# A batched matrix-vector product: longer pieces per load, y loaded once, one reduce in four moved to GpSimd and ScalarE

One core of a Trainium2 chip (trn2) is used. The metric is the device time of one execution in microseconds, lower is better.

## The reference

```python
def setup_inputs():
    batch, dim_i, dim_j = 32, 512, 1024
    return {"x": randn(batch, dim_i, dim_j) as float32, "y": randn(batch, dim_j) as float32}

def reference(x, y):
    return np.einsum('bij,bj->bi', x, y)          # float32
```

Each of the 32 x 512 results is a dot product of 1,024 elements. The input x has 67.1 MB and each of its elements is used once, so the time cannot be shorter than reading x takes.

## The kernel before

```python
    xp = ctx.enter_context(tc.tile_pool(name="xp", bufs=12))
    yrowp = ctx.enter_context(tc.tile_pool(name="yrowp", bufs=4))
    ybcp = ctx.enter_context(tc.tile_pool(name="ybcp", bufs=3, space=PSUM))
    # ... (cut)
    for b in range(B):
        yrow = yrowp.tile([1, J], fp32)
        nc.sync.dma_start(out=yrow, in_=y[b : b + 1, :])
        ybc = ybcp.tile([P, J], fp32)                 # y[b] on all 128 partitions
        for h in range(J // MM_FREE):
            nc.tensor.matmul(ybc[:, sl], lhsT=ones, rhs=yrow[:, sl], start=True, stop=True)
        for t in range(IT):                           # 4 tiles of 128 rows
            xt = xp.tile([P, J], fp32)
            eng = x_dma_engines[(b * IT + t) % 2]     # SyncE and ScalarE in turn
            eng.dma_start(out=xt, in_=x[b, t * P : (t + 1) * P, :])
            nc.vector.tensor_tensor_reduce(out=scratch, in0=xt, in1=ybc, op0=mult, op1=add,
                                           accum_out=res_sb[:, col : col + 1])   # ... (cut)
    nc.tensor.transpose(res_T_psum, res_sb, identity)  # then one copy and one store
```

A load has 512 KB, one row (4 KB) per partition. A reduce multiplies a tile by the broadcast y and sums along the row, on VectorE.

## Time and profile before

| | before |
|---|---|
| time, median of 15 runs | 180.3 us (179.97 to 181.2) |
| span in the profile | 178.7 us |
| VectorE busy | 157.4 us in 257 instructions |
| rate of the stream in most slices | 408 to 411 GB/s |

The lines are shown and read in the prediction below. In the page of a profile, the first part gives the busy time of each engine (DVE is VectorE, ACT ScalarE, POOL GpSimd, PE TensorE, PEld its weight loads). The second gives each in 40 equal slices of the span, and the bytes per second in the row GB/s. A line of part 5 is a group of equal instructions: line of code, engine, operation, output <- inputs, shapes, count | busy us, mean ns of one | idle us before them and what ended most of it.

### The profile page before, as it was taken

The page shows a single profiled execution, that of the slowest core. Times are in us where ns is not written, and L with a number is a line of the kernel's source. Part 1 is how long each engine was busy: PE and PEld are TensorE (multiplying, and loading weights), DVE is VectorE, ACT ScalarE, POOL GpSimd, SP SyncE. Part 2 cuts the span into 40 slices and gives each one's busy share as a digit, 9 for nine tenths or more (in the row PEclk, how much of TensorE's full clock was granted, in tenths as well). Part 3 has the DMA queues.
Part 4 walks back from the last instruction along what each step waited for, and adds up shares of the span by engine and source line. Part 5 has one row for each costly group of instructions (what it writes and reads, how often), then busy time and mean ns, then how long its engine had stood idle before and what let it go on. Part 6 is the DMA issues. An engine that isn't in the chain of part 4 may idle for free. (4 is left out here: it accounts for less than half of the span.)

```text
span 178.7 us, 1032 instructions
## 1 busy us (share of the span) xinstructions
PE 119.6 (67%) x129; PEld 37.5 (21%) x129; DVE 157.4 (88%) x257; ACT 1.5 (1%) x2; POOL 0.7 (0%) x6
## 2 busy tenths in 40 slices
PE   2586666787666688666678766667969898666001
PEld 1122211122211122221112222221314232111000
DVE  0379899999999999999999999999999999999992
ACT  0000000000000000000000000000000000002000
POOL 1000000000000000000000000000000000000000
DMA  5999999999999999999999999999999999999800
GB/s 182 423 412 409 408 409 409 411 409 408 411 408 410 409 411 411 409 410 410 408 407 402 388 413 401 370 393 415 408 405 364 391 372 409 406 414 409 319 6 15
DMA packets 18646, 67.37 MB, mean 377 GB/s; under 512 B 2096, under 2 KB 2224, under 8 KB 18640
## 3 DMA queue, kind: packets, MB, share of 16 engines
q1 hardware_dynamic: 9424, 33.76, 47.9%
q10 hardware_dynamic: 9216, 33.56, 47.5%
q14 instruction: 5, 0.04, 0.1%
q8 instruction: 1, 0.02, 0.0%
HBM read 67.24 MB, written 0.07 MB: 377 GB/s over the span
## 5 line engine op out<-in xcount | busy, mean ns | idle before, releaser
L68 DVE CUSTOM_DVE_ANT_0 scratch<-xt,ybc 128x1024 f32<-128x1024 f32 x128 | 156.2, 1221 | 17.2 <-PE ybc L55 12.7
L55 PE MATMUL ybc<-yrow,ones 1*128 1x512 f32 x128 | 119.1, 1087 | 44.7 <-DMA yrow<-in_y_dram 41.1
L55 PEld LDWEIGHTS ybc<-yrow,ones 1*128 1x128 f32 x128 | 37.3, 319 | 124.9 <-issue 113.4
L68 DVE DVE_READ_ACCUMULATOR2_ANT res_sb<- 128x1 f32 x128 | 10.5, 82 | 0.0
L80 PE MATMUL res_T_psum<-identity,res_sb 128*128 128x128 f32 x1 | 0.4, 447 | 11.7 <-DVE res_sb L68 11.7
L80 PEld LDWEIGHTS res_T_psum<-identity,res_sb 128*128 128x128 f32 x1 | 0.2, 183 | 13.3 <-issue 13.3
L82 ACT ACT_TABLE_LOAD x1 | 1.3, 1283 | 160.9 <-DMA xt<-in_x_dram 160.9
L40 DVE MEMSET ones<- 1x128 f32 x1 | 0.2, 165 | 0.8 <-PEq L99 0.8
L82 ACT COPY res_T_sb<-res_T_psum 128x128 f32<-128x128 f32 x1 | 0.3, 266 | 13.8 <-PE res_T_psum L80 13.8
masks.py:199 POOL TENSOR_SCALAR_AFFINE_SELECT identity<-identity 128x128 f32<-128x128 f32 x1 | 0.3, 294 | 0.1
masks.py:197 POOL MEMSET identity<- 128x128 f32 x1 | 0.2, 206 | 0.3 <-POOLq L99 0.3
L99 POOL MEMSET const-bfloat16-1.0<- 128x1 bf16 x1 | 0.1, 102 | 0.0
L99 POOL MEMSET const-uint8-127<- 128x1 uint8 x1 | 0.1, 102 | 0.0
L99 POOL MEMSET const-float32-0.0<- 128x1 f32 x1 | 0.1, 99 | 0.2 <-issue 0.2
L99 POOL MEMSET const-float32-1.0<- 128x1 f32 x1 | 0.1, 99 | 0.0
## 6 DMA issues: line engine op xcount, KB each, us to landing
xt<-in_x_dram ACTq DMA_DIRECT2D x64, 512.0 KB
xt<-in_x_dram SPq DMA_DIRECT2D x64, 512.0 KB
yrow<-in_y_dram SPq DMA_DIRECT2D x32, 4.0 KB
out_dram<-res_T_sb SPq DMA_DIRECT2D x1, 64.0 KB
```

The lines of the kernel that those rows point to most:

```text
L40: nc.vector.memset(ones, 1.0)
L55: nc.tensor.matmul(ybc[:, sl], lhsT=ones, rhs=yrow[:, sl], start=True, stop=True,)
L68: nc.vector.tensor_tensor_reduce(out=scratch, in0=xt, in1=ybc, scale=1.0, scalar=0.0, op0=mybir.AluOpType.mult, op1=mybir.AluOpType.add, a ...
L80: nc.tensor.transpose(res_T_psum, res_sb, identity)
L82: nc.scalar.copy(res_T_sb, res_T_psum)
L99: nc = _bacc.Bacc("TRN2", target_bir_lowering=False, num_devices=1)
```

## The change

The intent is to take time from all three things that the loop is made of. Loads become 2 MB, with four consecutive rows (16 KB) per partition. The whole of y is loaded once, and a column of the identity picks the row to broadcast. One of the four reduces of a batch is done as a product on GpSimd and a sum on ScalarE. The last batch keeps 512 KB loads.

```diff
-    xp = ctx.enter_context(tc.tile_pool(name="xp", bufs=12))
+    PACK = 4;  TAIL = 1;  OFFLOAD = 1
+    packs = [PACK] * (B - TAIL) + [1] * TAIL
+    xp = ctx.enter_context(tc.tile_pool(name="xp", bufs=7))
+    yall = consts.tile([B, J], fp32)
+    nc.sync.dma_start(out=yall, in_=y)
...
-                lhsT=ones,
-                rhs=yrow[:, sl],
+                lhsT=identity[0:B, b : b + 1].broadcast_to([B, P]),
+                rhs=yall[:, sl],
+        off = OFFLOAD if b < B - 1 else 0
+        if off:
+            nc.scalar.copy(ysb, ybc)                  # a copy of y in SBUF for GpSimd
...
-            eng.dma_start(out=xt, in_=x[b, t * P : (t + 1) * P, :])
+            src = x[b, t * P * pack : (t + 1) * P * pack, :].rearrange("(p r) j -> p r j", r=pack)
+            nc.sync.dma_start(out=xt, in_=src)
+                if u < off:
+                    nc.gpsimd.tensor_tensor(prod, xt[:, k, :], ysb, mult)
+                    nc.scalar.activation(junk, prod, Copy, accum_out=res_sb[:, col : col + 1])
+                else:
+                    nc.vector.tensor_tensor_reduce(...)   # as before
...
+        if b == g1 - 1:        # groups of up to 8 batches: 4 transposes, 4 strided copies, one store
```

More of the change, by code (lines that the diff above doesn't have):

```diff
@@ L23 @@
     P = 128
-    IT = I // P
-    assert I % P == 0
-    NCOL = B * IT
+    UNITS = I // P
     MM_FREE = 512
+    PACK = 4
+    TAIL = 1
+    OFFLOAD = 1
+    packs = [PACK] * (B - TAIL) + [1] * TAIL
+    groups, start = [], 0
+    for b in range(1, B + 1):
+        if b == B or packs[b] != packs[start] or (b - start) == 8:
+            groups.append((start, b))
+            start = b
     consts = ctx.enter_context(tc.tile_pool(name="consts", bufs=1))
-    xp = ctx.enter_context(tc.tile_pool(name="xp", bufs=12))
-    yrowp = ctx.enter_context(tc.tile_pool(name="yrowp", bufs=4))
+    xp = ctx.enter_context(tc.tile_pool(name="xp", bufs=7))
     ybcp = ctx.enter_context(tc.tile_pool(name="ybcp", bufs=3, space=bass.MemoryType.PSUM))
+    ysbp = ctx.enter_context(tc.tile_pool(name="ysbp", bufs=3))
+    prodp = ctx.enter_context(tc.tile_pool(name="prodp", bufs=3))
     scratchp = ctx.enter_context(tc.tile_pool(name="scratchp", bufs=1))
-    resp = ctx.enter_context(tc.tile_pool(name="resp", bufs=1))
-    outp = ctx.enter_context(tc.tile_pool(name="outp", bufs=1))
-    outpsum = ctx.enter_context(tc.tile_pool(name="outpsum", bufs=1, space=bass.MemoryType.PSUM))
-    ones = consts.tile([1, P], fp32)
-    nc.vector.memset(ones, 1.0)
+    outsbp = ctx.enter_context(tc.tile_pool(name="outsbp", bufs=2))
+    outpsum = ctx.enter_context(tc.tile_pool(name="outpsum", bufs=2, space=bass.MemoryType.PSUM))
+    yall = consts.tile([B, J], fp32)
+    nc.sync.dma_start(out=yall, in_=y)
     identity = consts.tile([P, P], fp32)
@@ L44 @@
     scratch = scratchp.tile([P, J], fp32)
-    res_sb = resp.tile([P, NCOL], fp32)
-    x_dma_engines = [nc.sync, nc.scalar]
+    junk = scratchp.tile([P, J], fp32)
+    res_sb = consts.tile([P, B * UNITS], fp32)
+    gi = 0
+    out_sb = None
     for b in range(B):
-        yrow = yrowp.tile([1, J], fp32)
-        nc.sync.dma_start(out=yrow, in_=y[b : b + 1, :])
-        ybc = ybcp.tile([P, J], fp32)
+        pack = packs[b]
+        ybc = ybcp.tile([P, J], fp32, name=f"ybc{b}", tag="ybc")
         for h in range(J // MM_FREE):
@@ L61 @@
             )
-        for t in range(IT):
-            xt = xp.tile([P, J], fp32)
-            eng = x_dma_engines[(b * IT + t) % len(x_dma_engines)]
-            eng.dma_start(out=xt, in_=x[b, t * P : (t + 1) * P, :])
-            col = b * IT + t
-            nc.vector.tensor_tensor_reduce(
-                out=scratch,
-                in0=xt,
-                in1=ybc,
-                scale=1.0,
-                scalar=0.0,
-                op0=mybir.AluOpType.mult,
-                op1=mybir.AluOpType.add,
-                accum_out=res_sb[:, col : col + 1],
-            )
@@ L79 @@
-    res_T_psum = outpsum.tile([P, NCOL], fp32)
-    nc.tensor.transpose(res_T_psum, res_sb, identity)
-    res_T_sb = outp.tile([P, NCOL], fp32)
-    nc.scalar.copy(res_T_sb, res_T_psum)
-    out_view = out.rearrange("b (t p) -> (b t) p", p=P)
-    nc.sync.dma_start(out=out_view, in_=res_T_sb)
+        off = OFFLOAD if b < B - 1 else 0
+        if off:
+            ysb = ysbp.tile([P, J], fp32, name=f"ysb{b}", tag="ysb")
+            nc.scalar.copy(ysb, ybc)
+        g0, g1 = groups[gi]
+        if b == g0:
+            out_sb = outsbp.tile([8, I], fp32, name=f"outsb{gi}", tag="outsb")
@@ new lines @@
+        for t in range(UNITS // pack):
+            xfull = xp.tile([P, PACK, J], fp32, name=f"x{b}_{t}", tag="x")
+            xt = xfull[:, 0:pack, :]
+            src = x[b, t * P * pack : (t + 1) * P * pack, :].rearrange("(p r) j -> p r j", r=pack)
+            nc.sync.dma_start(out=xt, in_=src)
+            for k in range(pack):
+                u = t * pack + k
+                col = b * UNITS + u
+                if u < off:
+                    prod = prodp.tile([P, J], fp32, name=f"prod{b}_{u}", tag="prod")
+                    nc.gpsimd.tensor_tensor(prod, xt[:, k, :], ysb, mybir.AluOpType.mult)
+                    nc.scalar.activation(
+                        junk, prod, mybir.ActivationFunctionType.Copy,
+                        accum_out=res_sb[:, col : col + 1],
+                    )
+                else:
+                    nc.vector.tensor_tensor_reduce(
+                        out=scratch,
+                        in0=xt[:, k, :],
+                        in1=ybc,
+                        scale=1.0,
+                        scalar=0.0,
+                        op0=mybir.AluOpType.mult,
+                        op1=mybir.AluOpType.add,
+                        accum_out=res_sb[:, col : col + 1],
+                    )
@@ new lines @@
+        if b == g1 - 1:
+            G = g1 - g0
+            tr_ps = outpsum.tile([8, UNITS, P], fp32, name=f"trps{gi}", tag="trps")
+            for u in range(UNITS):
+                nc.tensor.transpose(
+                    tr_ps[:G, u, :], res_sb[:, g0 * UNITS + u : g1 * UNITS : UNITS], identity
+                )
+                t_, k_ = divmod(u, pack)
+                c0 = P * pack * t_ + k_
+                nc.scalar.copy(
+                    out_sb[0:G, c0 : c0 + pack * (P - 1) + 1 : pack], tr_ps[:G, u, :]
+                )
+            nc.scalar.dma_start(out=out[g0:g1, :], in_=out_sb[:G, :])
+            gi += 1
```

## The prediction

> **What bounds the kernel now.** I read the page first (busy shares, the row of slices, the groups), then the table of windows, then the waits of the engines, then the timeline of the last 20 us.
>
> ```profile
> PE 119.6 (67%) x129; PEld 37.5 (21%) x129; DVE 157.4 (88%) x257; ACT 1.5 (1%) x2; POOL 0.7 (0%) x6
> DMA  5999999999999999999999999999999999999800
> GB/s 182 423 412 409 408 409 409 411 409 408 411 408 410 409 411 411 409 410 410 408 407 402 388 413 401 370 393 415 408 405 364 391 372 409 406 414 409 319 6 15
> DMA packets 18646, 67.37 MB, mean 377 GB/s; under 512 B 2096, under 2 KB 2224, under 8 KB 18640
> ...
> L68 DVE CUSTOM_DVE_ANT_0 scratch<-xt,ybc 128x1024 f32<-128x1024 f32 x128 | 156.2, 1221 | 17.2 <-PE ybc L55 12.7
> L55 PE MATMUL ybc<-yrow,ones 1*128 1x512 f32 x128 | 119.1, 1087 | 44.7 <-DMA yrow<-in_y_dram 41.1
> L55 PEld LDWEIGHTS ybc<-yrow,ones 1*128 1x128 f32 x128 | 37.3, 319 | 124.9 <-issue 113.4
> L68 DVE DVE_READ_ACCUMULATOR2_ANT res_sb<- 128x1 f32 x128 | 10.5, 82 | 0.0
> ```
>
> The DMA row is full from slice 1 to slice 36, at 408 to 411 GB/s in most slices. In the later half some fall to 364 to 402. VectorE is nearly as full. Two resources of almost the same length therefore run side by side. The input alone is 32 x 512 x 1024 x 4 B = 67.1 MB, and 67.1 MB at 410 GB/s is 163.7 us. VectorE has 128 reduces, and the timeline shows what each really occupies:
>
> ```profile
> 171.65 1.22 DVE L68 CUSTOM_DVE_ANT_0 scratch<-xt,ybc 128x1024 f32<-128x1024 f32 x1
> 172.79 0.08 DVE L68 DVE_READ_ACCUMULATOR2_ANT res_sb<- 128x1 f32 x1
> 172.91 1.22 DVE L68 CUSTOM_DVE_ANT_0 scratch<-xt,ybc 128x1024 f32<-128x1024 f32 x1
> ...
> 174.17 1.22 DVE L68 CUSTOM_DVE_ANT_0 scratch<-xt,ybc 128x1024 f32<-128x1024 f32 x1
> 175.32 0.08 DVE L68 DVE_READ_ACCUMULATOR2_ANT res_sb<- 128x1 f32 x1
> 175.54 0.45 PE L80 MATMUL res_T_psum<-identity,res_sb 128*128 128x128 f32 x1 [11.74 <-DVE res_sb L68]
> 176.03 0.27 ACT L82 COPY res_T_sb<-res_T_psum 128x128 f32<-128x128 f32 x1 [13.81 <-PE res_T_psum L80]
> ```
>
> The starts 171.65, 172.91 and 174.17 lie 1.26 us apart (1.262 in the longest row of them); 128 x 1.262 = 161.5 us. First reduce at 7.12 us, last one done at 175.4.
>
> The windows show when the bytes stop:
>
> ```profile
> 140.00:160.00 20.00, 15.91 (x18) 4.64 (x16) 19.15 (x32) 0.00 (x0) 0.00 (x0) 1.00 1.01 397
> 165.00:167.00 2.00, 0.00 (x0) 0.00 (x0) 1.83 (x5) 0.00 (x0) 0.00 (x0) 1.00 1.03 410
> 167.00:169.00 2.00, 0.00 (x0) 0.00 (x0) 1.95 (x4) 0.00 (x0) 0.00 (x0) 1.00 0.85 338
> 169.00:171.00 2.00, 0.00 (x0) 0.00 (x0) 1.85 (x3) 0.00 (x0) 0.00 (x0) 1.00 0.10 39
> ```
>
> The columns are PE, PEld, DVE, ACT, POOL, clock, DMA share and GB/s. The data is in at about 168.9 us, yet VectorE, which was busy 19.15 of the 20 us before that, goes on to 175.4 without a gap: it ends 6.5 us, five reduces, behind the transfers. It fell behind at the start and at batch borders (12.7 us waiting for the broadcast product, which waited 41.1 us for its 4 KB row of y, queued behind the big loads). So the end is set by VectorE, and the stream of bytes is only a few us shorter.
>
> **What the Trainium skill says.** (1) "DMA: Bandwidth & Descriptors", section Where 436 GB/s comes from: the SBUF side of the 16 engines carries 435 GB/s at most. Its section Why small descriptors are slow gives a fixed cost per packet. The trace agrees with both: its packet records have a median of 159 ns for the 4,096 B packets of x and 307 ns for the 8,192 B packets of the instruction queue. So 148 ns go per 4 KB and 11 ns are fixed; 4,096 B / 159 ns x 16 = 412 GB/s, which is the slice value. (2) "SBUF — State Buffer", section Who interferes with whom: a VectorE instruction with at most one SBUF input, outside the two-port modes, does not contend with GpSimd. The reduce here reads x from SBUF and the broadcast from PSUM, so it should not; no run here shows it yet. (3) "GPSIMD Engine Reference", section 3.1: 4,497 ns for a two-input fp32 product of 2,048 columns. Half of it is an estimate of 2.3 us for 1,024. GpSimd does nothing comparable in this trace. (4) "VectorE: DVE Perf Modes", section The TRN2 errata: ScalarE takes 172 + columns cycles from PSUM, 224 + columns from SBUF, at 1.2 GHz. For the 128-column copy of this trace that gives 250 ns against 266 measured, so it fits.
>
> **The change, part by part.**
>
> *Loads.* 128 loads of 512 KB become 31 of 2 MB, four consecutive rows per partition, and four of 512 KB for the last batch. Each partition's piece is contiguous on both sides: 16 KB in place of 4 KB. If it travels as one packet, a packet costs 4 x 148 + 11 = 603 ns (estimate from the packet records), 27.2 GB/s per engine, 434 GB/s for 16. I take 430 for ragged edges, since before gets 409 to 411 out of 412. 67.1 MB / 430 = 156.1 us in place of 163.7. The loads are issued from one queue only; one issue took 0.33 us against 4.9 us of transfer, so this costs nothing. Seven 2 MB buffers (14 MB) against twelve of 512 KB (6 MB) let the queue run ahead.
>
> *Reduces.* One of four in 31 batches leaves VectorE: 128 - 31 = 97 remain, 97 x 1.262 = 122.4 us. Per batch VectorE needs 3 x 1.262 = 3.8 us and the transfer 4.9. VectorE stops being a bound. GpSimd gets 31 products of about 2.3 us (71 us in all). ScalarE gets 31 broadcasts copied from PSUM, (172 + 1024) / 1.2 = 1.0 us, and 31 summing passes, (224 + 1024) / 1.2 = 1.04 us and some 0.2 for the accumulator: about 2.2 us per batch, 70 us in all. Each fits into 4.9 us.
>
> *y.* 32 rows of 4 KB become one load of 128 KB ahead of everything. The row of the identity, broadcast, selects batch b, so the same 128 matmul records of 1.09 us stay, but nothing waits for a y row behind 10 us of queued x. The 12.7 us of VectorE waits and the 41.1 us of PE waits vanish.
>
> *Output.* One transpose, one copy and one store become five groups of four transposes, four strided copies and a store. Four groups lie beside the stream. The last group (one batch) has its first three transposes beside the reduces; after the last reduce come one transpose, one copy and a store as before: 175.4 to 178.7, 3.3 us.
>
> *The sum.* The first x byte moves about 0.4 us later than before, since y is issued first: about 2.8 us. Plus 156.1 gives the last byte at 158.9. The last 2 MB load (batch 30) lands whole, about 4.9 us before that, and its three reduces run until 3.8 us later. The four tiles of batch 31 then follow without gaps: 7 x 1.262 = 8.8 us after batch 30 landed, hence 3.9 us after the last byte. With 3.3 us for transpose, copy and store the span is 158.9 + 3.9 + 3.3 = 166.1. Times stand 1.7 us above the span (180.45 for the profiled run of 178.7), so 167.8 us.
>
> **Rivals.**
>
> *The packets stay at 4 KB.* If descriptors are still cut at a row, the rate stays at 410 and the stream ends at 2.8 + 163.7 = 166.5; 166.5 + 7.2 + 1.7 = 175.4 us. For it: every x packet before is 4 KB. Against it: 8 KB packets occur in the same trace, and four rows are contiguous on both sides. I give it one in four.
>
> *A new wait at the group border.* If PE takes instructions in the order of the text, batch 31's broadcast comes behind the four transposes of batches 24 to 30, which need batch 30's last reduce. These transposes share a PSUM bank with the copies that read them, so they alternate: 4 x (0.45 + 0.27 + some wait) is about 3 us. Then come four matmul records (3.75 us in the timeline of the first batch). The four last reduces would start about 10.4 us after batch 30 landed instead of 3.8: plus 6.6 us, so 174.4. Earlier borders have the same stall, but seven buffers absorb it. Against it: the instruction order need not be that of the text, since the product depends only on y. I give this three in ten; with the first rival 182 us.
>
> *GpSimd and VectorE block each other.* If each product shut VectorE out for 2.3 us, a batch would take 3.8 + 2.3 = 6.1 us on VectorE: 195 us for 32. The skill's rule speaks against it; under one in ten.
>
> *The offload buys nothing.* If the rate stays at 410, VectorE (5.05 us a batch) would nearly keep pace without help, and most of the gain is from y and the end. That lies inside the first rival.
>
> **Range and chances.** Main case, about half: 168. One rival alone: 174 to 175, about four in ten. Both, or port contention: 182 or more. The floor of 435 GB/s gives 2.8 + 154.3 + 7.2 + 1.7 = 166. I put 168.5, since a small part of the border wait may appear, with a range of 165.5 to 177.0. Faster by 2% means under 176.7.
>
> **What would show it.** Packets of x of 16 KB and slices at 425 to 435 GB/s; if 408 to 411, the first rival. VectorE idle about a fifth of each slice, waiting for x and not for the broadcast. A reduce of 1,221 ns still; if its mean grows, the engines contend. The last reduce about 4 us after the last byte; if 10, with VectorE waiting for PE at batch 31, the second rival. GpSimd products near 2.3 us; above 4.9 it is the bound and everything here is wrong.

## The result

171.44 us (171.01 to 171.5, 8 runs) against 180.3. The ratio is 0.9502, with a 95% interval of 0.9489 to 0.9515. Here and below a ratio is the mean time of one kernel's runs over that of the other's of the same rounds, so it is not quite the ratio of the medians quoted. Executions over 1.5% slower than the fastest of the same kernel are left out of the means. The forecast was 168.5, range 165.5 to 177.0: right, and 2.9 us too low.

The page of the profile after (parts 1, 2 and 5):

```profile
span 169.3 us, 902 instructions
PE 125.3 (74%) x148; PEld 39.5 (23%) x148; DVE 119.2 (70%) x194; ACT 72.5 (43%) x114; POOL 73.8 (44%) x37
...
GB/s 151 434 434 434 430 426 430 430 430 418 430 426 424 434 434 434 430 434 420 422 426 430 426 422 434 434 434 422 434 422 422 424 436 428 420 426 405 359 11 4
DMA packets 5157, 67.36 MB, mean 398 GB/s; under 512 B 608, under 2 KB 608, under 8 KB 1184
...
L91 DVE CUSTOM_DVE_ANT_0 scratch<-x,ybc 128x1024 f32<-128x1024 f32 x97 | 118.4, 1221 | 47.2 <-DMA x<-in_x_dram 33.2
...
L85 POOL TENSOR_TENSOR prod<-x,ysb 128x1024 f32<-128x1024 f32 x31 | 73.1, 2356 | 85.4 <-DMA x<-in_x_dram 59.5
L71 ACT COPY ysb<-ybc 128x1024 f32<-128x1024 f32 x31 | 31.2, 1005 | 49.2 <-PE ybc L61 48.9
L86 ACT ACTIVATE junk<-prod 128x1024 f32<-128x1024 f32 x31 | 32.8, 1059 | 33.5 <-POOL prod L85 33.2
```

The stream went from about 410 to between 418 and 436 GB/s. There are 5,157 packets in place of 18,646, and 5,157 - 1,184 = 3,973 of them have 8 KB or more. 31 loads x 128 partitions are 3,968, so each partition's 16 KB travels as one packet. VectorE now waits for x. Its reduce takes 1,221 ns as before, so GpSimd's products beside it did not lengthen it.

The timeline of the end (start us, length us, engine, line, operation, output <- inputs):

```profile
151.56 3.74 PE L61 MATMUL ybc<-yall,identity 32*128 32x512 f32 x4 [1.42 <-DVE res_sb L91]
...
157.45 2.36 POOL L85 TENSOR_TENSOR prod<-x,ysb 128x1024 f32<-128x1024 f32 x1 [2.55 <-DMA x<-in_x_dram]
157.45 1.22 DVE L91 CUSTOM_DVE_ANT_0 scratch<-x,ybc 128x1024 f32<-128x1024 f32 x1 [1.14 <-DMA x<-in_x_dram]
...
161.04 0.38 PE L105 MATMUL trps<-identity,res_sb 128*7 128x128 f32 x1 [5.74 <-ACT junk L86]
...
165.13 1.22 DVE L91 CUSTOM_DVE_ANT_0 scratch<-x,ybc 128x1024 f32<-128x1024 f32 x1
...
166.53 0.37 PE L105 MATMUL trps<-identity,res_sb 128*1 128x128 f32 x1 [0.34 <-ACT outsb L110]
166.94 0.26 ACT L110 COPY outsb<-trps 1x128 f32<-1x128 f32 x1 [0.46 <-PE trps L105]
167.22 0.23 ACTq L113 DMA_DIRECT2D out_dram<-outsb  x1
```

Batch 30, the last 2 MB load, is there at 157.45. Seven reduces follow, the last done at 166.37, then transpose, copy and store. The broadcast for batch 31 was made at 151.56, ahead of the border's transposes at 161.04: the order on TensorE is not that of the text.

### The profile page after: what moved, and what is told of

Same layout as the page of the kernel before. It is cut to its first block, busy times and chain, and to the rows that moved or that the text cites.

```text
span 169.3 us, 902 instructions
## 1 busy us (share of the span) xinstructions
PE 125.3 (74%) x148; PEld 39.5 (23%) x148; DVE 119.2 (70%) x194; ACT 72.5 (43%) x114; POOL 73.8 (44%) x37
## 2 busy tenths in 40 slices
DMA packets 5157, 67.36 MB, mean 398 GB/s; under 512 B 608, under 2 KB 608, under 8 KB 1184
## 5 line engine op out<-in xcount | busy, mean ns | idle before, releaser
L91 DVE CUSTOM_DVE_ANT_0 scratch<-x,ybc 128x1024 f32<-128x1024 f32 x97 | 118.4, 1221 | 47.2 <-DMA x<-in_x_dram 33.2
L61 PE MATMUL ybc<-yall,identity 32*128 32x512 f32 x128 | 118.4, 1084 | 25.3 <-DVE res_sb L91 21.9
L85 POOL TENSOR_TENSOR prod<-x,ysb 128x1024 f32<-128x1024 f32 x31 | 73.1, 2356 | 85.4 <-DMA x<-in_x_dram 59.5
L61 PEld LDWEIGHTS ybc<-yall,identity 32*128 32x128 f32 x128 | 37.9, 321 | 97.4 <-issue 93.2
L71 ACT COPY ysb<-ybc 128x1024 f32<-128x1024 f32 x31 | 31.2, 1005 | 49.2 <-PE ybc L61 48.9
L86 ACT ACTIVATE junk<-prod 128x1024 f32<-128x1024 f32 x31 | 32.8, 1059 | 33.5 <-POOL prod L85 33.2
L105 PE MATMUL trps<-identity,res_sb 128*8 128x128 f32 (+2 forms) x20 | 7.4, 380 | 16.4 <-ACT junk L86 9.4
L110 ACT COPY outsb<-trps 8x128 f32<-8x128 f32 (+2 forms) x20 | 7.1, 354 | 11.3 <-PE trps L105 10.9
L91 DVE DVE_READ_ACCUMULATOR2_ANT res_sb<- 128x1 f32 x97 | 7.9, 82 | 0.0
L86 ACT ACTIVATION_READ_ACCUMULATOR junk<-prod 128x1 f32 x31 | 5.9, 190 | 0.0
## 6 DMA issues: line engine op xcount, KB each, us to landing
x<-in_x_dram SPq DMA_DIRECT2D x31, 2048.0 KB, 30.4
```

The costliest lines, as they stand in the source:

```text
L61: nc.tensor.matmul(ybc[:, sl], lhsT=identity[0:B, b : b + 1].broadcast_to([B, P]), rhs=yall[:, sl], start=True, stop=True,)
L71: nc.scalar.copy(ysb, ybc)
L85: nc.gpsimd.tensor_tensor(prod, xt[:, k, :], ysb, mybir.AluOpType.mult)
L86: nc.scalar.activation(junk, prod, mybir.ActivationFunctionType.Copy, accum_out=res_sb[:, col : col + 1],)
L91: nc.vector.tensor_tensor_reduce(out=scratch, in0=xt[:, k, :], in1=ybc, scale=1.0, scalar=0.0, op0=mybir.AluOpType.mult, op1=mybir.AluOpTy ...
L105: nc.tensor.transpose(tr_ps[:G, u, :], res_sb[:, g0 * UNITS + u : g1 * UNITS : UNITS], identity)
```

## The experiments

All twelve gave correct results. Each was compared with the kernel before, run in the same rounds (its median was 179.95 to 180.04 there). The verdict asks whether the ratio, with its 95% interval, shows a change of 2%. In the four runs of the first group (y_at_once to small_loads) the kernel before scattered from 179.87 to 182.38 us, so their intervals reach 0.007 to 0.008 to either side; elsewhere it is 0.002 or less.

| kernel | us | ratio to before |
|---|---|---|
| before | 180.0 | 1 |
| y_at_once: only y | 178.78 | 0.9898 |
| no_offload: y and packets | 178.41 | 0.9879 |
| y_rows_back: packets and offload | 178.02 | 0.9858 | unclear |
| small_loads: y and offload | 175.92 | 0.9736 | unclear |
| after: all three (other rounds) | 171.44 | 0.9502 |
| rows_apart | 177.97 | 0.9883 |
| pack2 | 171.93 | 0.9548 |
| tail2 | 170.99 | 0.9496 |
| head1_tail2 | 170.83 | 0.9485 |
| tail2_own | 170.64 | 0.9483 |
| end_offload2 | 172.29 | 0.9575 |
| best | 170.01 | 0.9447 |
| tail3_one_copy | 169.84 | 0.9434 |

The theory: before, VectorE and the stream were almost equally long and VectorE had lost some us to late y rows; the change shortens the stream by longer packets and takes VectorE out of the way. The main rivals: one part makes nearly all of the gain; or the size of a load counts and not that of a packet.

### One part alone, and one part undone

**y_at_once.** To the kernel before:

```diff
-        yrow = yrowp.tile([1, J], fp32)
-        nc.sync.dma_start(out=yrow, in_=y[b : b + 1, :])
+    yall = consts.tile([B, J], fp32)           # ahead of the loop
+    nc.sync.dma_start(out=yall, in_=y)
-                lhsT=ones,            rhs=yrow[:, sl],
+                lhsT=identity[0:B, b : b + 1].broadcast_to([B, P]),  rhs=yall[:, sl],
```

> The kernel before with only its y loaded at once and selected by the identity; 512 KB loads of 4 KB packets, all 128 reduces on VectorE, single output. My theory (VectorE and the stream were almost equal, and VectorE lost its time to late y rows): VectorE runs from 7.1 us without gaps, 7.1 + 128 x 1.262 + 3.3 + 1.7 = 173.6; the stream at 410 GB/s allows about the same. So 174 us, two thirds of the whole gain from y alone. Rival (the gain of the change is that of the larger packets, y is a side matter): 178 to 180.

Measured: 178.78 us. My 174 was a miss. Two lines of its waits (engine, line, what it waited for: us in total, times, longest) and its timeline show why:

```profile
DVE scratch L65 <- PE ybc L52: 7.6, 1, 7.6
DVE scratch L65 <- DMA xt<-in_x_dram: 1.0, 2, 0.7
```
```profile
7.61 1.22 DVE L65 CUSTOM_DVE_ANT_0 scratch<-xt,ybc 128x1024 f32<-128x1024 f32 x1 [7.61 <-PE ybc L52]
...
11.40 1.22 DVE L65 CUSTOM_DVE_ANT_0 scratch<-xt,ybc 128x1024 f32<-128x1024 f32 x1
...
12.75 1.22 DVE L65 CUSTOM_DVE_ANT_0 scratch<-xt,ybc 128x1024 f32<-128x1024 f32 x1
...
28.20 1.22 DVE L65 CUSTOM_DVE_ANT_0 scratch<-xt,ybc 128x1024 f32<-128x1024 f32 x1
```

The waits for y are gone but the one at the start. Yet the first reduce of a batch starts 1.35 us after the one before it, not 1.26. Four batches take 28.20 - 7.61 = 20.59 us, 5.15 each, so 32 take 164.7 us and not the 161.5 that I had worked out from 128 equal steps. 7.6 + 164.7 = 172.3; two small waits, the store and the 1.7 us beside the span make up the rest. The kernel before was therefore much nearer to its VectorE bound than I thought: of 175.4 us up to its last reduce, 7.1 + 164.7 = 171.8 were start and work, and only about 3.6 were waiting.

**no_offload.** To the kernel after:

```diff
-    OFFLOAD = 1
+    OFFLOAD = 0
```

> The kernel after with all 128 reduces on VectorE. My theory: VectorE is the bound again, from the first landing at 9.2 us without gaps: 9.2 + 161.5 + 2.9 + 1.7 = 175.3. So the offload is worth about 4 us, but only because the first landing is late and the stream is fast. Rival (the stream alone sets the time, GpSimd and ScalarE help nothing): 171.4.

Measured: 178.41 us. With the corrected 164.7 us of work the sum is 9.2 + 164.7 + 2.9 + 1.7 = 178.5, which it is. The stream was through by 160 us, and VectorE was idle for 16.4 us, 9.0 of them before the first landing:

```profile
GB/s 156 442 434 420 427 442 434 416 431 431 425 431 427 427 434 434 420 420 434 434 431 418 425 434 438 427 421 420 431 434 423 427 423 438 431 384 132 0 3 0
...
L91 DVE CUSTOM_DVE_ANT_0 scratch<-x,ybc 128x1024 f32<-128x1024 f32 x128 | 156.2, 1221 | 16.4 <-DMA x<-in_x_dram 9.0
```

So the offload is worth 178.4 - 171.4 = 7.0 us beside long packets. With 4 KB packets it is about 178.8 - 175.9 = 2.9 us (y_at_once against small_loads, which differ a little in more than that: buffers, queues and output).

**small_loads.** To the kernel after:

```diff
-    PACK = 4
+    PACK = 1
-    xp = ... bufs=7
+    xp = ... bufs=28
```

> The kernel after with one row per partition in every load (512 KB, 4 KB packets, 28 buffers, so the same memory); y at once and the offload stay. My theory: slices fall to 410 GB/s, last byte near 168, but the end shrinks, since the last reduce then comes 1.3 us after the last load instead of 3.9: 168 + 1.3 + 2.9 + 1.7 = 174. If only the stream counted, 171.4 + 5.5 = 177. Rival (packet size is nothing, the offload and y are everything): 171.

Measured: 175.92 us. The slices fell to 410 GB/s as expected. Nearly 2 us more than my 174 were lost, and some of it is in two slices where the stream itself stopped for a while (363 and 332 GB/s):

```profile
GB/s 194 376 416 416 409 412 408 409 410 410 405 410 411 410 409 410 407 408 410 410 408 411 399 414 410 410 410 402 413 409 408 363 332 407 416 410 410 408 243 4
```
```profile
SPq L79 <- DMA out_dram<-outsb: 14.7, 3, 5.1
```

The second line is from the waits of the queue that issues the loads: three loads waited 14.7 us in total for a store of the output. The loads were queued less far ahead than in the kernel after (median 10.2 us from issue to landing, against 30.4), so such a wait can reach the stream. That these waits caused the two slices was not tested.

**y_rows_back.** To the kernel after:

```diff
-    nc.sync.dma_start(out=yall, in_=y)
+        yrow = yrowp.tile([1, J], fp32)                  # in the loop, 4 buffers
+        nc.sync.dma_start(out=yrow, in_=y[b : b + 1, :])
```

> The kernel after with the 32 separate row loads of y put back, each issued ahead of its batch on the same queue. My theory: with 2 MB loads y of a batch lands a whole load (4.9 us) before its x, and the broadcast takes 3.75 us, so it is ready just before x: no wait, 171.4 within 1 us. Rival (late y rows cost 6 us here as they did before): 177.

Measured: 178.02 us, so the rival's number, and my "no wait" fell. But it is not the wait of before. Its waits and a part of its timeline:

```profile
POOL prod L88 <- ACT ysb L74: 75.5, 27, 4.8
ACT junk L89 <- POOL prod L88: 74.6, 31, 4.3
DVE scratch L94 <- ACT ysb L74: 38.4, 28, 3.4
```
```profile
142.65 0.99 ACT L74 COPY ysb<-ybc 128x1024 f32<-128x1024 f32 x1
...
143.77 2.36 POOL L88 TENSOR_TENSOR prod<-x,ysb 128x1024 f32<-128x1024 f32 x1 [2.21 <-ACT ysb L74]
...
146.16 1.06 ACT L89 ACTIVATE junk<-prod 128x1024 f32<-128x1024 f32 x1 [2.52 <-POOL prod L88]
...
147.22 0.99 ACT L74 COPY ysb<-ybc 128x1024 f32<-128x1024 f32 x1
148.25 1.22 DVE L94 CUSTOM_DVE_ANT_0 scratch<-x,ybc 128x1024 f32<-128x1024 f32 x1 [0.82 <-ACT ysb L74]
```

Copy, product, sum and the next copy form a ring, for ScalarE copies the next y only after the sum of this batch. One turn takes 147.22 - 142.65 = 4.57 us, and a load takes 4.94. VectorE hangs on the ring too: it starts a batch only after ScalarE's copy, although it reads ybc itself. The skill's page "PSUM — Partial Sum Buffer", section Terms, says that two engines on the same bank and quadrant of PSUM at once are an error, reads against reads included; the wait of 38.4 us fits a program that keeps the two apart. A ring with 0.4 us of slack per batch hardly makes up for a delay, and when the last bytes came (by about 161 us) the work was behind; the last reduce started at 172.18. In the kernel after, y is early, a copy can be made before x is there, and VectorE waits only 10.4 us for ScalarE's sums and 1.2 for its copies. That the ring is at work is in the trace; where its first delay comes from I did not settle. The ring is not the whole loss either. The last reduce starts 7.05 us later than in the kernel after (172.18 against 165.13); 4.8 of these were lost when batch 30's reduces began (162.28 against 157.45). At 168.39 VectorE then waited 2.35 us more for TensorE, which made the second half of batch 31's broadcast (166.28) only after the border's first transpose (165.97). That is the border wait of the prediction's second rival, in a small form.

Together: two of the three parts give 1.6 to 4.1 us, all three 8.9. After any two of them something else is almost as long as what was shortened. The longer packets alone and the offload alone were not run, and the new grouping of the output was not undone by itself.

### Packet or load

**rows_apart.** To the kernel after; the same 2 MB loads, but the four rows of a partition lie 128 rows apart:

```diff
-            src = ....rearrange("(p r) j -> p r j", r=pack)
+            src = ....rearrange("(r p) j -> p r j", r=pack)
```

> The kernel after with the same 2 MB loads, but the four rows of a partition 128 rows apart in memory, so each row is a piece of 4 KB. Tells load size from packet size. My theory (the fixed 11 ns per packet): packets of 4 KB, slices of 410 GB/s, a batch every 5.12 us in place of 4.94; 30 x 0.18 = 5.4 more, so 176 to 177, longer than with small 4 KB loads since the late 2 MB batch keeps its 3.9 us end. Rival (the size of a load counts): 171.4.

Measured: 177.97 us, and the stream is that of before:

```profile
GB/s 153 400 396 418 410 413 407 412 409 409 410 409 408 411 410 409 409 410 410 409 411 409 411 409 410 409 410 407 412 408 410 409 413 407 409 409 409 382 19 1
DMA packets 17061, 67.36 MB, mean 382 GB/s; under 512 B 608, under 2 KB 608, under 8 KB 17056
```

For the rate, the load size is not what counts; the contiguous piece is. It cost a us more than expected: batches came 5.17 us apart, not 5.12 (first landing 9.51 us, batch 30 at 164.50). And it is slower than small_loads, since the end keeps the batch that lands as a whole.

**pack2.** To the kernel after:

```diff
-    PACK = 4            # 7 buffers
+    PACK = 2            # 14 buffers
```

> The kernel after with two rows per partition in a load (1 MB, 8 KB packets, 14 buffers). My theory: packets near 310 ns, so 8,192 B / 310 ns x 16 = 423 GB/s less 1%, stream 1 to 1.5 us longer; first landing earlier by about a us; the end shorter by one reduce (six in place of seven after the last large load). Together 170.5 to 171.5, about the same as after. Rival (only 16 KB packets reach the fast rate, 8 KB stay at 410): 175.

Measured: 171.93 us (ratio 0.9548), half a us worse than after and just outside the 170.5 to 171.5. The packet records of the packed traces have medians of 159 ns for 4 KB, 312 for 8 KB and 614 for 16 KB. About 152 ns per 4 KB and 7 ns per packet fit all three; the 148 and 11 of the prediction, from a handful of 8 KB packets, give 307 and 603. In rate, 8 KB packets bring about half of the gain: 8,192 B / 312 ns x 16 = 420 GB/s, against 412 and 427. In time they bring nearly all of it. The earlier first landing and the shorter end, which the expectation names, may make up the rest; they were not separated.

### The end

**tail2**, and **tail2_own**, which gives the small loads buffers of their own:

```diff
-    TAIL = 1
+    TAIL = 2
+    xsp = ctx.enter_context(tc.tile_pool(name="xsp", bufs=8))     # tail2_own only
```

> The kernel after with the last two batches, not one, in loads of 512 KB. My theory: of the time after the last byte, 3.9 us is VectorE working off batch 30, which lands as a whole; with small loads its reduces follow the tiles and the last one comes 1.3 us after the last landing; the stream gets 0.2 us longer. 171.4 - 2.6 + 0.2 = 169.0. Rival (the end is set by the offload chain or by the transposes of the border, not by VectorE's queue): 171.4.

> As tail2, with buffers of their own for the small loads of the end, which in tail2 waited for 2 MB buffers while the stream fell to 338 GB/s. Tells apart why tail2 gained 0.4 us and not 2.4. Theory now (VectorE's queue): after batch 29 lands at 152.6, ten reduces of 1.26 follow without a gap, as in tail2 (last one done at 165.5), however early the tiles land: 171.0 again, with the stream full to its end. Rival (the starved stream at the end): 169.5.

Measured: 170.99 and 170.64 us, where after had 171.44 (ratios 0.9496, 0.9483, 0.9502). The 169.0 was a miss: 0.4 us came and not 2.4, and by the ratios tail2 cannot be told from after. I had let the last reduce follow the last tile, and forgotten to count VectorE's queue. Batch 29 lands as a whole at 152.5, and from there ten reduces are to be done, 12.8 us, while the tiles come in 10. The last reduces of tail2_own:

```profile
152.54 1.22 DVE L94 CUSTOM_DVE_ANT_0 scratch<-x,ybc 128x1024 f32<-128x1024 f32 x1 [1.20 <-DMA x<-in_x_dram]
...
164.10 1.22 DVE L94 CUSTOM_DVE_ANT_0 scratch<-xs,ybc 128x1024 f32<-128x1024 f32 x1
```

The second run told the two explanations apart. With own buffers the stream at the end stayed at 408 GB/s between 155 and 160 us, where tail2 had 338; the last reduce ended at 165.3 in place of 165.5. A starved stream was there, but it was not what set the end.

**head1_tail2.** As tail2, and the first batch in small loads:

```diff
+    packs = [1] + [PACK] * (B - TAIL - 1) + [1] * TAIL
```

> As tail2, and the first batch too in loads of 512 KB. The first 16 KB packets took up to 1.7 us and the first slices moved fewer bytes than in the kernel before. My theory: that is the cost of starting with long packets, and with 4 KB packets first the stream starts about 0.5 us fuller: 168.5. Rival (the slow start is that of y ahead of x on one queue): as tail2.

Measured: 170.83 us, against 170.99 for tail2 in the same rounds: nothing that can be told from noise. The windows (engines' busy time, clock, DMA share, GB/s), first for after, then for head1_tail2:

```profile
2.50:5.00 2.50, 1.63 (x2) 0.83 (x3) 0.00 (x0) 0.00 (x0) 0.00 (x0) 1.00 0.73 249
5.00:20.00 15.00, 14.36 (x18) 5.27 (x17) 8.38 (x13) 6.24 (x8) 5.76 (x3) 1.00 1.02 435
```
```profile
2.50:5.00 2.50, 2.03 (x3) 1.01 (x4) 0.00 (x0) 0.00 (x0) 0.00 (x0) 1.00 0.95 362
5.00:20.00 15.00, 13.03 (x18) 4.03 (x16) 8.00 (x13) 5.78 (x10) 5.36 (x3) 1.00 1.02 421
```

The stretch from 2.5 to 5 us is fuller, but nothing is gained: with the first 2.5 us (125 and 77 GB/s), both kernels had moved some 7.4 to 7.5 MB by 20 us. Nor are long packets shown to be the cause of the slow stretch. rows_apart, with 2 MB loads of 4 KB packets, has 303 GB/s there, and small_loads, with 512 KB loads of the same packets, 374. So the size of the loads seems to matter at the start; the cause stays open.

**end_offload2.** To the kernel after:

```diff
-        off = OFFLOAD if b < B - 1 else 0
+        off = 2 if b == B - 2 else OFFLOAD if b < B - 1 else 0
```

> The kernel after with two reduces of batch 30, not one, done by GpSimd and ScalarE; all loads as they were. Theory (VectorE's queue after the last large load): six reduces in place of seven follow the landing of batch 30, 1.26 us less: 170.2. Rival (the end is bound by the stream): 171.4. If the second product comes too late for the transposes, more than 171.4.

Measured: 172.29 us (ratio 0.9575), slower than after. This is the third case that I had named. Its last reduce starts at 164.43, but the store is issued at 168.75:

```profile
162.73 1.06 ACT L86 ACTIVATE junk<-prod 128x1024 f32<-128x1024 f32 x1 [1.17 <-POOL prod L85]
163.78 0.36 ACT L110 COPY outsb<-trps 7x128 f32<-7x128 f32 x1
...
164.43 1.22 DVE L91 CUSTOM_DVE_ANT_0 scratch<-x,ybc 128x1024 f32<-128x1024 f32 x1
...
168.47 0.26 ACT L110 COPY outsb<-trps 1x128 f32<-1x128 f32 x1 [0.46 <-PE trps L105]
168.75 0.23 ACTq L113 DMA_DIRECT2D out_dram<-outsb  x1
```

The second sum ends near 164, ScalarE gets to the border's copies only then, and eight transposes and copies in turn follow. Shortening VectorE's queue made ScalarE the end.

**best.** tail2_own with the first batch small, y issued by ScalarE, and the second offloaded reduce one load earlier:

```diff
-    nc.sync.dma_start(out=yall, in_=y)
+    nc.scalar.dma_start(out=yall, in_=y)
+        off = 2 if b == B - 3 else OFFLOAD if b < B - 1 else 0
```

> All together: first batch and last two batches in 512 KB loads with eight buffers of their own, y on ScalarE's queue so that x is issued first, two reduces of batch 29 offloaded. Theory: the start 0.5 to 0.9 us earlier, nine reduces in place of ten after batch 29, so the last one comes about one reduce after the last tile: 171.4 - 2.3 - 0.7 = 168.4. If the queue of VectorE were not the end's bound: 170 to 171.

**tail3_one_copy.** best with three small batches at the end, 6 large and 12 small buffers, the second offload in batch 28, and one strided copy per border:

```diff
+    TAIL = 3
+            if b < B - 1:
+                view = "g (p u) -> g u p" if pack == PACK else "g (u p) -> g u p"
+                nc.scalar.copy(out_sb[0:G, :].rearrange(view, u=UNITS), tr_ps[:G, :, :])
```

> The kernel best with a third batch at the end in 512 KB loads (12 small buffers, 6 of 2 MB), the two offloaded reduces in batch 28, and each border's four transposes followed by one strided copy in place of four in turn (the last group keeps four). Theory (VectorE's queue and the alternating transposes and copies set the end): 12 reduces of 1.27 after batch 28 lands at about 148, so the last reduce ends near 163.6 instead of 164.7, and the store follows it by 3.0 instead of 3.4 us; 168.5. Rival (stream and store are all that is left): 170.0.

Measured: 170.01 us (0.9447, 0.9434 to 0.9460) and 169.84 (0.9434, 0.9421 to 0.9447): best is faster than both given kernels, its interval lying below that of after (0.9489 to 0.9515), by about 0.6%. Both expectations were misses. For best 168.4 was forecast, and the number of its rival came. Its start was not earlier: on ScalarE's queue y came later (first broadcast at 4.70 us, 3.37 in after), and the first reduce waited for ScalarE's copy of it until 9.53 us (9.23 in after). For tail3_one_copy 168.5 was forecast; it cannot be told from best. Its VectorE waits 1.30 us for a tile and starts again at 155.85; seven reduces follow at 1.26 to 1.36 us, which is also the pace of the tiles (512 KB at 409 GB/s is 1.28 us), and the last one ends at 164.8, where best has 164.7. VectorE has no queue left there, so the stream and the store after it are what remains; that is a reading of the trace and was not tested further.

## Why the prediction was right

Its main case was 167.8 us and the number 168.5; 171.44 was measured. The range also held either rival alone (174 to 175), so the time by itself does not show the mechanism. The trace does: packets of 16 KB, reduces of 1,221 ns, VectorE waiting mostly for x, seven reduces after batch 30. Sizes were off. The terms of its sum:

| term | predicted | in the trace after |
|---|---|---|
| first 2 MB landed | 2.8 + 4.9 = 7.7 us | 9.2 |
| 30 more loads | 30 x 4.88 = 146.3 | 157.45 - 9.23 = 148.2, 4.94 each |
| seven reduces | 8.8 | 8.9 |
| transpose, copy, store | 3.3 | 2.9 |
| span to time | 1.7 | 1.7 |

- *"The last 2 MB load (batch 30) lands whole, about 4.9 us before that."* This was the largest miss. The sum let loads land strictly one after the other. The windows of after up to the first landing, and from the landing of batch 30 on, show that they overlap:

```profile
0.00:9.23 9.23, 5.86 (x7) 2.50 (x8) 0.00 (x1) 2.29 (x2) 0.71 (x7) 1.00 0.81 300
157.45:169.30 11.85, 2.86 (x8) 0.60 (x8) 8.60 (x14) 3.67 (x10) 2.35 (x1) 1.00 0.26 102
```

  By 9.23 us 2.77 MB had moved, though y and the first load are 2.23 MB. After batch 30 had landed, only 1.2 MB were still to come, where the sum left the 2.1 MB of batch 31. The missing 0.9 MB are about 2.1 us at 428 GB/s.
- *"The first x byte moves about 0.4 us later"* and *"I take 430."* The rest, about 1.3 us, is a slower start (249 GB/s between 2.5 and 5 us, 365 in before) and a stream of 428 GB/s between the two landings; a 16 KB packet takes 614 ns and not 603. The first two rows of the table, 3.4 us together, cover the whole error of the span (169.3 against 166.1), less 0.3 that the end was shorter.
- *The packets stay at 4 KB.* Rejected by the packet counts; rows_apart shows what it would have cost.
- *A new wait at the group border.* Rejected for the kernel after: the broadcast of batch 31 came first. In y_rows_back a wait of this kind took 2.35 us. And the alternation of transposes and copies that I described is real, at 0.85 us a pair, and in end_offload2 it set the end.
- *GpSimd and VectorE block each other.* Rejected: 1,221 ns in both kernels. A product takes 2,356 ns (2.3 us estimated; the page's 4,497 ns, which the prediction calls a product, is for an add), copy and sum 1,005 and 1,059 ns, with 190 ns for reading the accumulator.
- *"128 x 1.262 = 161.5 us."* Wrong by 3.2 us, since each batch border costs 0.09 us more. This did not touch the forecast, as VectorE is no bound after the change, but it touched the reasons: I thought that late y rows cost more and the offload less than they did. Also, 6.1 of the 12.7 us that were to vanish were the wait for the first broadcast, which stays at the start. y alone is worth 1.3 us (0.6 to 3.1 by the interval of its ratio), and the offload beside long packets 7.0.
- *The offload buys nothing* at 410 GB/s. Not quite: about 2.9 us.

## What to carry to other kernels

When a stream and an engine are almost equally long, shortening one of them shows little; work out both bounds with the real step between instructions, borders included, and expect the gain only when both move. For a stream, look at the packets: here the contiguous piece on each side set the rate, not the size of a load. At the end, count what is still queued when the last large load lands, because an engine works it off after the last byte; do not take that landing from the byte count alone (here it came 2.1 us later). Then look at which engine has to hand over the result.

## What the Trainium skill lacked or had wrong

- "DMA: Bandwidth & Descriptors", sections Measured and Rules for kernel authors, gives its advice in bytes per DMA (at least 1 MiB). Here 2 MB loads made of 4 KB pieces ran at 410 GB/s, as 512 KB loads do, and 2 MB loads of 16 KB pieces at 428. The page has no time for packets of these sizes: 159, 312 and 614 ns for 4, 8 and 16 KB.
- The same page says that a packet has preferably at most 4,096 B (section SWDGE vs HWDGE vs iDMA, in a table on the descriptors that GpSimd builds). It gives no size for loads issued from SyncE; here these had packets of 16 KB.
- No page that I read has the slow start of a stream of large loads: from 2.5 to 5 us, 249 GB/s with 2 MB loads of 16 KB packets and 303 with 2 MB loads of 4 KB packets, against 374 with 512 KB loads of 4 KB packets.
- "VectorE: DVE Perf Modes" has no figure for a reduce that also reads its accumulator: 1,221 ns for 1,024 columns with one input from PSUM, 1.26 us from start to start, and 1.35 us for the first one of a batch.
- "GPSIMD Engine Reference", section 3.1, was near for a product of half the size: half of its 4,497 ns (for an add of 2,048 columns) is 2.25 us, 2.356 measured. "SBUF — State Buffer", section Who interferes with whom, was right that a reduce with one SBUF input does not contend with GpSimd (1,221 ns with and without it).
